# Second layer: 32 tokens gather the rows of their own experts, and work on gathered rows keeps its program order

## The chip, the cores and the metric

The kernel runs on one core of a Trainium2 chip as one launch. Its time is device microseconds (us); lower is better. Of the core's engines the text needs TensorE (PE in the profile, with its weight loads as PEld), VectorE (DVE), ScalarE (ACT), GpSimd (POOL, which issues the gathers) and SyncE (SP, a queue that issues loads). Sixteen DMA engines move data between HBM and the on-chip memory.

## What is computed

The model is two layers over 256 latent tokens (and, in the first layer, 256 context tokens). Each layer is a set of attention-like mixers and then an expert network, and it is the expert network that the change touches. Each token scores 8 x 2 x 128 keys, picks 128 of 16,384 experts (16 for each of 8 heads), and gets

```python
def peer_ffn(h, wq, sub_keys, u, v):
    ...
        fs, fpos = lax.top_k(cand_s, PEER_TOPK)
        eidx = jnp.take_along_axis(cand_i, fpos, axis=-1)
        gate = jax.nn.softmax(fs, axis=-1)
        act = jax.nn.gelu(jnp.einsum('td,thkd->thk', xb, u[eidx]).astype(F32), approximate=False)
        w = (gate * act).astype(xb.dtype)
        return jnp.einsum('thk,thkd->td', w, v[eidx])
```

Here `u` and `v` are tables of 16,384 rows of 1024 floats (64 MB each) for each layer. The first layer runs 512 tokens through this network, the second 256.

## The kernel before

There are two ways to do the expert network, and the kernel uses both.

**The dense way** computes every expert for every token and multiplies by a gate that is zero for the experts not chosen. The 16,384 experts are 128 blocks of 128. In the *u stage* (`u_blocks`, called in pairs by `u_pair`) each block of `u` is loaded (tile `raw`, 1 MB for two blocks, two buffers), split into a high part by a ScalarE copy and a low part by a VectorE subtraction (tiles `spl`, a ring of ten), and multiplied with the split activations `h2h`, `h2l`: eight chunks of the 1024 features, each as three fp32r products (`mm3`, lines 72 to 74), 24 products per block, into a PSUM tile `pu`. The moving operand has one column per token: `self.wd[l]` columns, 384 in the first layer and 256 in the second. A gelu goes to DRAM (`ad`), or for the first 40 blocks of the second layer stays in `kept`. In the *v stage* (`v_blocks`) the same is done with `v`: 128 blocks, again 24 products each of `wd[l]` columns, accumulated over all blocks in eight PSUM tiles `f0` to `f7`; the moving operand there is activation times gate (`va`, split into `wh` and `wl`).

The gate matrix is built while the u stage runs: `route` decodes which experts a token chose, and for groups of 8 tokens `gate_hot` builds one-hot tiles on VectorE (`bt`, `eq`, two `at`) and `gates` multiplies them on TensorE (tile `pg`, 16 fp16 products per group).

**The gathered way** (`tokens_apart`) takes only the 128 experts of each token. In the first layer, 128 tokens (one per partition) are set apart: for each of 128 slots a POOL indirect DMA gathers one row per partition (128 x 1024 floats, 512 KB), VectorE multiplies with the token's activation `ht` and sums (a *dot*, line 1384), and later another gather of `v` rows is scaled and added to `facc` (an *addition*, line 1391). In the u stage the gathered rows share the ring `spl`; in the v stage they have a ring `row` of four. The generator is advanced by `rows_to`: `PHASE1` steps are spread over the u stage, the rest over the first 58 pairs of the v stage. The second layer sets no tokens apart.

What sets the order: a scheduler places each engine's instructions by priority and by when it believes operands are ready. `pin` adds an edge that keeps an instruction behind everything written before it on its engine; it may still be placed later. Each engine then executes its list strictly in that order, so an instruction that waits holds up all behind it.

Of the kernel before, what the change touches and what calls it, by code (L numbers as in the profile page):

```python
# [18 lines left out]
L = 2  # L19
KD = 8  # L20
# [16 lines left out]
APART = 128  # L37
ROWS = 4
PHASE1 = 168
# [14 lines left out]
class Kernel:  # L54
# [39 lines left out]
    def build(self):  # L94
        tc, nc, A = self.tc, self.nc, self.A
        with ExitStack() as es:
# [25 lines left out]
            self.wd = [TA - APART, TC]  # L122
# [911 lines left out]
    def peer(self, l):  # L1034
# [5 lines left out]
        apart = (w - wd) // 128  # L1040
        with ExitStack() as es:
# [19 lines left out]
            with ExitStack() as e1:  # L1061
# [4 lines left out]
                with ExitStack() as e2:  # L1066
# [14 lines left out]
                    with self.order("DVE", "Activation"):  # L1081
                        self.pin(self.whigh(wr[0], ws[0], h0))
                        self.whigh(wr[0], ws[0], h1)
                        self.pin(self.wlow(wr[0], ws[0], h0))
                        scr = self.s.tile([128, 512], F32, name="s")
                        self.rs_diag(w, 1024, self.ms, scr)
                        self.wlow(wr[0], ws[0], h1)
                        self.norm2(aff, ts, hh, hl, self.rs_mm(w, scr, self.psum.tile([128, 512], F32, name="mm")), ht=ht)
# [10 lines left out]
                with ExitStack() as e2:  # L1099
# [12 lines left out]
                    if apart:  # L1112
                        for n, _ in enumerate(routes[0]):
                            if n % RN[l] == 0:
                                u_pair()
                        sp = self.tokens_apart(l, fin[0], ht)
                        next(sp)
                    first = apart
# [7 lines left out]
                    def u_next():  # L1126
                        u_pair()
                        rows_to(PHASE1 * (used[0] - u0) // (64 - u0))
                    for n, _ in enumerate(routes[first]):
                        if n % RN[l] == 0:  # L1130
                            u_next()
                    nd = nt - first
                    cost = [GW if t + 1 < nd else 1.0 for t in range(nd) for _ in range(16)]
                    left = 64 - used[0] - GL[l]
                    done = 0
                    sl = self.gate_slots(fin[first])
                    hot = self.gate_hot(sl, 0)
# [3 lines left out]
                    for x in range(16 * nd):  # L1141
                        t, g = divmod(x, 16)
                        while done < int(left * sum(cost[:x + 1]) / sum(cost) + 1e-6):
                            u_next()
                            done += 1
                        cur = hot
                        if t + 1 < nd:
                            next(routes[first + t + 1], None)
                            if g == 14:
                                for _ in routes[first + t + 1]:  # L1150
                                    pass
                                sl2 = self.gate_slots(fin[first + t + 1])
                            if g == 15:
                                sl = sl2
                        if x + 1 < 16 * nd:
                            hot = self.gate_hot(sl, (g + 1) % 16)
                        self.gates(l, t, g, cur)
# [4 lines left out]
                with ExitStack() as e2:  # L1162
# [16 lines left out]
                    for n, i in enumerate(self.v_order(l)):  # L1179
                        rows_to(PHASE1 + (256 - PHASE1) * n // 58 if n < 58 else 300)  # L1180
                        self.v_blocks(l, n, i, acc, ts, w - wd)
                        if extra:
                            self.ada_row(self.vp, *extra.pop(0))
# [3 lines left out]
    def norm2(self, aff, ts, hh, hl, rs, ks=range(KD), ht=None):  # L1187
# [12 lines left out]
        for k in ks:  # L1200
# [8 lines left out]
            if ht is not None:  # L1209
# [3 lines left out]
                nc.tensor.transpose(pt[:, c], t[:, 0:128], self.ident)  # L1213
                if k % 4 == 3:
                    nc.scalar.copy(ht[:, (k - 3) * 128:(k + 1) * 128], pt)
# [122 lines left out]
    def gates(self, l, t, g, hot):  # L1338
# [6 lines left out]
        for q in range(2):  # L1345
# [7 lines left out]
            if nf:  # L1353
                o = t * 128 + g * 8 + 4 * q
                f = self.kept[:, :, o:o + 4]
                nc.vector.scalar_tensor_tensor(f, pg[:, :nf], 1.0 / GSCALE, f, op0=ALU.mult, op1=ALU.mult)
        if g % 4 == 3:
            nc.scalar.dma_start(self.gd[l][4 * t + g // 4][:, nf:], self.gst)

    def tokens_apart(self, l, fin, ht):  # L1360
# [3 lines left out]
        ix = far.tile([128, 128], U32, name="ix")  # L1364
        fx = far.tile([128, 128], F32, name="fx")
        nc.vector.scalar_tensor_tensor(fx, fin[:, 0], 128.0, fin[:, 1], op0=ALU.mult, op1=ALU.add)
        nc.vector.tensor_copy(ix, fx)
        ga = far.tile([128, 128], F32, name="ga")
        nc.vector.tensor_copy(ga, fin[:, 2])
        dots = far.tile([128, 128], F32, name="dots")  # L1370
        wt = far.tile([128, 128], F32, name="wt")
        junk = self.junk = far.tile([128, 1024], F32, name="junk")
        self.facc = far.tile([128, 1024], F32, name="facc")
        tabs = [self.A[n].rearrange("a b d -> (a b) d") for n in (f"un{l}", f"vn{l}")]
# [5 lines left out]
        C = 16  # L1380

        def dot(s):
            r = gather(0, s)
            nc.vector.scalar_tensor_tensor(junk, r, 1.0, ht, op0=ALU.mult, op1=ALU.mult, accum_out=dots[:, s:s + 1])

        def add(s):
            r = gather(1, s)
            if s == 0:
                nc.vector.tensor_scalar(self.facc, r, wt[:, 0:1], None, op0=ALU.mult)
            else:  # L1390
                nc.vector.scalar_tensor_tensor(self.facc, r, wt[:, s:s + 1], self.facc, op0=ALU.mult, op1=ALU.add)
        yield
        for c in range(0, 128 + C, C):
            for s in range(c, c + C):
                if s < 128:
# [5 lines left out]
            if c < 128:  # L1401
# [48 lines left out]
    def v_blocks(self, l, n, i, acc, ts, off):  # L1450
# [41 lines left out]
        if off:  # L1492
# [6 lines left out]
        with self.order("PE", "DVE", "Activation"):  # L1499
# [3 lines left out]
            for d in range(KD):  # L1503
                mm(d, 1)
                if off:
                    nc.tensor.transpose(acc[d][:, 0:128], self.facc[:, d * 128:(d + 1) * 128], self.ident)
# [196 lines left out]
def layout(inp):  # L1703
# [46 lines left out]
    d["un0"], d["vn0"] = (f[x][0].reshape(128, 128, 1024) for x in ("peer_u", "peer_v"))  # L1750
# [19 lines left out]
```

## Time and profile before

| what | value |
|---|---|
| median of 3 runs | 2875.59 us (2870.84 to 2876.46) |
| profiled execution, device time | 2874.08 us |
| its span | 2872.0 us, 47065 instructions |
| TensorE busy | 2701.9 us (94%) |
| VectorE busy | 2178.1 us (76%) |
| ScalarE busy | 1265.1 us (44%) |
| GpSimd busy | 389.9 us (14%) |
| DMA | 662.88 MB, mean 231 GB/s |

The profiled execution is 1.5 us below the median of the runs. The span covers, in order: mixers of the first layer (to about 420 us), its expert network (to about 1765), mixers of the second layer (to about 2030), its expert network (to about 2865) and the output. A busy TensorE is not TensorE at its peak, since products overlap: the time that one product really costs is the distance between the starts of two that follow each other, called the pitch below.

### The profile page before, as it was taken

How to read it: one execution, taken by the hardware profiler on the slowest of the kernel's cores; microseconds unless marked ns; L12 is line 12 of the kernel's file. 1: busy time of each engine (PE TensorE's matmuls, PEld its weight loads, DVE VectorE, ACT ScalarE, POOL GpSimd, SP SyncE). 2: the span in 40 equal slices, each digit the busy share in tenths (PEclk: the TensorE clock that was granted, in tenths of full speed). 3: DMA queues.
4: the chain of work that ended last, by engine and by line, in shares of the span. 5: the costliest groups of instructions: out<-in, count | busy, mean ns of one | idle time of the engine just before them, and what ended most of it. 6: DMA issues, size and time to landing. Idle time of an engine off the chain costs nothing.

```text
span 2872.0 us, 47065 instructions
## 1 busy us (share of the span) xinstructions
PE 2701.9 (94%) x18199; PEld 2491.3 (87%) x18199; DVE 2178.1 (76%) x4703; ACT 1265.1 (44%) x2185; POOL 389.9 (14%) x354
## 2 busy tenths in 40 slices
PE   8989989999999987999999998988999999999998
PEld 5766758998888877999999997766999999999998
DVE  5665667689999976799999986655789767666665
ACT  5564644343344432343333334654545445444443
POOL 0010000004444343322222310000000000000000
PEclk9999899999999998999999999999999999999999
DMA  7111423237899999999999984211535766877774
GB/s 265 71 48 45 162 88 134 90 136 280 309 369 367 358 364 343 337 341 374 370 370 368 368 301 136 89 37 52 194 136 187 250 240 234 292 240 248 249 246 143
DMA packets 268752, 662.88 MB, mean 231 GB/s; under 512 B 16496, under 2 KB 146672, under 8 KB 258928
## 3 DMA queue, kind: packets, MB, share of 16 engines
q1 hardware_dynamic: 198688, 450.04, 45.0%
q0 software_dynamic: 36864, 134.23, 12.6%
q10 hardware_dynamic: 32976, 75.61, 6.9%
q8 instruction: 142, 2.33, 0.3%
q14 instruction: 82, 0.67, 0.1%
HBM read 585.37 MB, written 74.45 MB: 230 GB/s over the span
## 4 chain that ended last, share of the span: by engine, by line
PE 70%; DVE 16%; DMA 5%; issue 4%; ACT 3%; SPq 1%; POOL 0%; ACTq 0%; DVEq 0%; POOLq 0%
PE pu L72 8%; PE pu L74 8%; PE pu L73 8%; PE f L73 8%; PE f L74 8%; PE f L72 7%; PE fp L72 3%; PE fp L73 3%; PE fp L74 3%; PE pg L1349 2%; DVE junk L305 2%; DVE spl L1469 2%; PE mm L72 2%; PE mm L73 2%; PE mm L74 2%
## 5 line engine op out<-in xcount | busy, mean ns | idle before, releaser
L72 PE MATMUL pu<-h2h,spl 128*128 128x384 f32 (+1 forms) x2048 | 649.6, 317 | 39.4 <-ACT spl L1417 38.3
L73 PE MATMUL f<-wl,spl 128*128 128x384 f32 (+1 forms) x2048 | 635.3, 310 | 11.0 <-DVE wl L1476 11.0
L74 PE MATMUL pu<-h2h,spl 128*128 128x384 f32 (+1 forms) x2048 | 636.9, 313 | 8.2 <-DVE spl L1418 7.9
L73 PE MATMUL pu<-h2l,spl 128*128 128x384 f32 (+1 forms) x2048 | 639.4, 312 | 0.0
L74 PE MATMUL f<-wh,spl 128*128 128x384 f32 (+1 forms) x2048 | 629.2, 309 | 0.0
L72 PE MATMUL f<-wh,spl 128*128 128x384 f32 (+1 forms) x2048 | 511.7, 311 | 11.6 <-ACT wh L1475 8.4
L1468 ACT CAST spl<-raw 128x1024 fp32r<-128x1024 f32 x256 | 268.0, 1050 | 389.8 <-PE f L73 343.0
L72 PEld LDWEIGHTS pu<-h2h,spl 128*128 128x128 f32 x2048 | 393.0, 192 | 47.3 <-ACT spl L1417 44.0
L1469 DVE TENSOR_TENSOR spl<-raw,spl 128x1024 fp32r<-128x1024 f32 x256 | 312.6, 1225 | 158.8 <-ACT spl L1468 157.5
L1417 ACT CAST spl<-raw 128x1024 fp32r<-128x1024 f32 x256 | 266.6, 1049 | 343.1 <-PE pu L73 229.4
L73 PEld LDWEIGHTS f<-wl,spl 128*128 128x128 f32 x2048 | 389.7, 190 | 16.8 <-DVE wl L1476 16.1
L74 PEld LDWEIGHTS pu<-h2h,spl 128*128 128x128 f32 x2048 | 391.7, 191 | 12.7 <-DVE spl L1418 12.4
L1418 DVE TENSOR_TENSOR spl<-raw,spl 128x1024 fp32r<-128x1024 f32 x256 | 311.8, 1221 | 110.9 <-ACT spl L1417 108.8
L73 PEld LDWEIGHTS pu<-h2l,spl 128*128 128x128 f32 x2048 | 393.1, 192 | 0.3
L72 PEld LDWEIGHTS f<-wh,spl 128*128 128x128 f32 x2048 | 377.9, 190 | 16.1 <-ACT wh L1475 11.3
L74 PEld LDWEIGHTS f<-wh,spl 128*128 128x128 f32 x2048 | 389.2, 190 | 0.0
L418 DVE TENSOR_TENSOR spl<-raw,spl 128x512 fp32r<-128x512 f32 (+1 forms) x226 | 150.3, 704 | 72.7 <-ACT spl L414 62.5
L1435 ACT ACTIVATE act<-pu 128x384 f32<-128x384 f32 (+1 forms) x216 | 95.7, 443 | 218.7 <-PE pu L74 213.6
L1378 POOL DMA_INDIRECT spl<-in_un,ix x92 | 128.8, 1400 | 387.5 <-DVE fp L1246 244.0
L347 POOL TENSOR_TENSOR ms<-ms,mhalf 128x4 f32<-128x4 f32 (+1 forms) x5 | 4.8, 953 | 1264.1 <-DVE sq L345 833.9
L1475 ACT CAST wh<-va 128x384 fp32r<-128x384 f32 (+1 forms) x216 | 100.0, 467 | 168.5 <-PE f L74 79.5
L414 ACT CAST spl<-raw 128x512 fp32r<-128x512 f32 (+1 forms) x226 | 130.5, 629 | 76.8 <-PE fp L73 28.9
(305 smaller groups left out, 4547.6 us busy)
## 6 DMA issues: line engine op xcount, KB each, us to landing
raw<-in_ut SPq DMA_DIRECT2D x128, 1024.0 KB
raw<-in_v SPq DMA_DIRECT2D x128, 1024.0 KB
adaw<-in_wadat SPq DMA_DIRECT2D x56, 512.0 KB
ad<-act ACTq DMA_DIRECT2D x64, 384.0 KB
gd<-gstage ACTq DMA_DIRECT2D x12, 2048.0 KB
vg<-gd SPq DMA_DIRECT2D x32, 768.0 KB
va<-ad SPq DMA_DIRECT2D x64, 384.0 KB
raw<-in_win SPq DMA_DIRECT2D x22, 1024.0 KB
```

What stands on the lines that cost most here:

```text
L72: mm(ps, ah, bh, start=first, stop=False, **kw)
L73: mm(ps, ah, bl, start=False, stop=False, **kw)
L74: mm(ps, al, bh, start=False, stop=last, **kw)
L414: return self.nc.scalar.copy(p[0][o], w[:, o])
L418: return eng.tensor_tensor(p[1][o], w[:, o], p[0][o].bitcast(F32), op=ALU.subtract)
L1378: nc.gpsimd.indirect_dma_start(r, None, tabs[which], bass.IndirectOffsetOnAxis(ix[:, s:s + 1], 0))
L1417: self.pin(nc.scalar.copy(uh, self.u[:, n % 2]), n < 3)
L1418: self.pin(nc.vector.tensor_tensor(ul, self.u[:, n % 2], uh.bitcast(F32), op=ALU.subtract), n < 3)
L1435: nc.scalar.activation(a[:, b, :w], ps[:, :w], AF.Gelu)
L1468: nc.scalar.copy(vh, v[:, b])
L1469: nc.vector.tensor_tensor(vl, v[:, b], vh.bitcast(F32), op=ALU.subtract)
L1475: nc.scalar.copy(wh[:, :w], a[:, b, :w])
```

## The change

`APART` and `PHASE1` become a pair, one entry per layer. In the second layer the first 32 latent tokens are set apart. They fill the 128 partitions four times: partition 32q + t holds token t with slots 32q to 32q + 31, so there are 32 dots and 32 additions of 128 rows each (groups of 8 slots instead of 16). To get there, `ht` (32 rows) is copied three times by DMA, the routing result `fin` is rearranged into `own` by four DMAs, and the four partial sums are added at the end by a product with a 128 x 32 selection matrix `fsel`. All of these DMAs stand in SP's queue. The dense products of the second layer are then 224 columns wide, four groups of 8 tokens need no gate, and the activation and gate tiles in DRAM shrink likewise. In the first layer the last transposes of `facc` become products with the identity. In both layers each dot and each addition is pinned.

```diff
-APART = 128
+APART = (128, 32)
-PHASE1 = 168
+PHASE1 = (168, 26)
...
-            self.wd = [TA - APART, TC]
+            self.wd = [TA - APART[0], TC - APART[1]]
...
+                        for q in range(apart, 128, apart):
+                            nc.sync.dma_start(ht[q:q + apart], ht[0:apart])
...
-                nc.tensor.transpose(pt[:, c], t[:, 0:128], self.ident)
+                nc.tensor.transpose(pt[0:na, c], t[:, 0:na], self.ident)
...
+        if n < 128:
+            own = far.tile([128, 3, S], F32, name="own")
+            for q in range(128 // n):
+                nc.sync.dma_start(own[q * n:(q + 1) * n], fin[0:n, :, q * S:(q + 1) * S])
+            fin = own
+        self.fsel = self.ident
+        if n < 128:
+            self.fsel = far.tile([128, n], F32, name="fsel")
+            nc.vector.tensor_copy(self.fsel, self.ident[:, 0:n])
+            for q in range(n, 128, n):
+                nc.vector.tensor_add(self.fsel, self.fsel, self.ident[:, q:q + n])
...
-            nc.vector.scalar_tensor_tensor(junk, r, 1.0, ht, op0=ALU.mult, op1=ALU.mult, accum_out=dots[:, s:s + 1])
+            self.pin(nc.vector.scalar_tensor_tensor(junk, r, 1.0, ht, op0=ALU.mult, op1=ALU.mult, accum_out=dots[:, s:s + 1]))
...
-                nc.vector.scalar_tensor_tensor(self.facc, r, wt[:, s:s + 1], self.facc, op0=ALU.mult, op1=ALU.add)
+                self.pin(nc.vector.scalar_tensor_tensor(self.facc, r, wt[:, s:s + 1], self.facc, op0=ALU.mult, op1=ALU.add))
...
-                    nc.tensor.transpose(acc[d][:, 0:128], self.facc[:, d * 128:(d + 1) * 128], self.ident)
+                    nc.tensor.matmul(acc[d][:, 0:off], self.facc[:, d * 128:(d + 1) * 128], self.fsel, start=True, stop=True)
```

VectorE, v stage of the second layer, before (`spl` is the low part of a block, `wl` the low part of the weighted activations):

```order
L1469 TENSOR_TENSOR spl<-raw,spl 128x1024
L1476 TENSOR_TENSOR wl<-va,wh 128x256
L1474 TENSOR_TENSOR va<-va,vg 128x256 x2
L1469 TENSOR_TENSOR spl<-raw,spl 128x1024
L1476 TENSOR_TENSOR wl<-kept,wh 128x256
```

The same place in the changed kernel:

```order
L1399 SCALAR_TENSOR_TENSOR junk,dots<-row,ht 128x1024
L1484 TENSOR_TENSOR spl<-raw,spl 128x1024
L1491 TENSOR_TENSOR wl<-va,wh 128x224
L1484 TENSOR_TENSOR spl<-raw,spl 128x1024
L1491 TENSOR_TENSOR wl<-va,wh 128x224
L1489 TENSOR_TENSOR va<-va,vg 128x224 x2
L1484 TENSOR_TENSOR spl<-raw,spl 128x1024
L1491 TENSOR_TENSOR wl<-kept,wh 128x224
L1484 TENSOR_TENSOR spl<-raw,spl 128x1024
L1491 TENSOR_TENSOR wl<-kept,wh 128x224
L1406 SCALAR_TENSOR_TENSOR facc<-row,wt,facc 128x1024
```

Dots and additions now stand between the splits that feed TensorE; the first dot stands behind the split of block 55 of the u stage, the last addition behind that of block 126 of the v stage.

VectorE, v stage of the first layer, before (line 305 computes modulation rows of the next layer):

```order
L1474 TENSOR_TENSOR va<-va,vg 128x384 x2
L1469 TENSOR_TENSOR spl<-raw,spl 128x1024
L306 TENSOR_TENSOR mod_12303<-mod_12303,badat 128x2
L1384 SCALAR_TENSOR_TENSOR junk,dots<-row,ht 128x1024
L1476 TENSOR_TENSOR wl<-va,wh 128x384 x2
L305 SCALAR_TENSOR_TENSOR junk,mod_12303<-adaw,csb 128x1024
L1469 TENSOR_TENSOR spl<-raw,spl 128x1024
L305 SCALAR_TENSOR_TENSOR junk,mod_12303<-adaw,csb 128x1024
L1391 SCALAR_TENSOR_TENSOR facc<-row,wt,facc 128x1024
```

The same stage in the changed kernel:

```order
L1406 SCALAR_TENSOR_TENSOR facc<-row,wt,facc 128x1024
L1484 TENSOR_TENSOR spl<-raw,spl 128x1024
L305 SCALAR_TENSOR_TENSOR junk,mod_12303<-adaw,csb 128x1024
L1484 TENSOR_TENSOR spl<-raw,spl 128x1024
L1489 TENSOR_TENSOR va<-va,vg 128x384 x2
L305 SCALAR_TENSOR_TENSOR junk,mod_12303<-adaw,csb 128x1024
L1491 TENSOR_TENSOR wl<-va,wh 128x384 x2
L306 TENSOR_TENSOR mod_12303<-mod_12303,badat 128x2
L1399 SCALAR_TENSOR_TENSOR junk,dots<-row,ht 128x1024
L1406 SCALAR_TENSOR_TENSOR facc<-row,wt,facc 128x1024
```

The same instructions stand there in a more regular order; a dot moves by a few places, and the last addition goes from behind the split of block 116 to behind that of block 125.

SP, u stage of the second layer, in the changed kernel (`raw` are the loads of `u`):

```order
L1430 DMA raw_21530<-in_ut 128x2x1024
L1430 DMA raw_21594<-in_ut 128x2x1024
L1371 DMA own_21491<-fin0_19268 32x3x32 x4
L1430 DMA raw_21698<-in_ut 128x2x1024
L1430 DMA raw_21801<-in_ut 128x2x1024
```

The four rearranging DMAs wait for the routing result, and the loads of `u` stand behind them; before the change there were only loads of `u` there.

## Rows read from the trace of the kernel before

**Rows 1.** The page: busy engines, and the chain by engine.

```profile
PE 2701.9 (94%) x18199; PEld 2491.3 (87%) x18199; DVE 2178.1 (76%) x4703; ACT 1265.1 (44%) x2185; POOL 389.9 (14%) x354
...
PE 70%; DVE 16%; DMA 5%; issue 4%; ACT 3%; SPq 1%; POOL 0%; ACTq 0%; DVEq 0%; POOLq 0%
```

**Rows 2.** Second layer's stretches: length, busy PE, PEld, DVE, ACT, POOL, clock, DMA share, GB/s.

```profile
2120.00:2200.00 80.00, 80.00 (x667) 79.81 (x666) 73.44 (x278) 41.11 (x62) 0.00 (x0) 1.00 0.47 161
2360.00:2440.00 80.00, 80.00 (x754) 79.37 (x753) 60.00 (x91) 39.66 (x71) 0.00 (x0) 1.00 0.68 235
...
2640.00:2720.00 80.00, 80.00 (x669) 80.00 (x668) 49.97 (x75) 37.93 (x56) 0.00 (x0) 1.00 0.75 250
```

**Rows 3.** PE's largest wait in the second expert network: total, times, longest.

```profile
PE mm L356 <- DVE s L351: 3.9, 2, 2.1
```

**Rows 4.** PE in order of time: start, duration; second layer, first of 52 and last.

```profile
2599.77 0.28 PE L72 MATMUL f<-wh,spl 128*128 128x256 f32 x1
...
2605.89 0.28 PE L72 MATMUL f<-wh,spl 128*128 128x256 f32 x1
```

**Rows 5.** The same for the first layer, 384 columns, first of 15 and last.

```profile
553.30 0.34 PE L74 MATMUL pu<-h2h,spl 128*128 128x384 f32 x1
...
555.73 0.33 PE L73 MATMUL pu<-h2l,spl 128*128 128x384 f32 x1
```

**Rows 6.** PEld and PE in order of time: short moving operands.

```profile
14.24 0.52 PEld L285 LDWEIGHTS tp<-con,adarow 2*128 2x128 f32 x4 [0.44 <-issue]
...
551.78 1.50 PE L1236 MATMUL sk<-keys,s 128*128 128x128 f32 x12
...
2215.08 1.44 PE L1349 MATMUL pg<-at,bt 128*128 128x128 f16 x22
```

**Rows 7.** PE and PEld groups by line and form: busy, mean ns of one.

```profile
L72 PE MATMUL pu<-h2h,spl 128*128 128x256 f32 x1024 | 295.8, 289 | 0.0
...
L1236 PE MATMUL sk<-keys,s 128*128 128x128 f32 x192 | 25.9, 275 | 0.0
...
L1349 PEld LDWEIGHTS <-bt 128*128 128x128 f16 x1280 | 76.8, 99 | 24.2 <-issue 10.1 <-DVE at L1335 9.4 <-DVE bt L1332 0.6
...
L74 PEld LDWEIGHTS fp<-spl,s 128*128 128x128 f32 x128 | 24.6, 192 | 0.0
```

**Rows 8.** VectorE groups, second expert network: busy, mean ns of one.

```profile
L1335 DVE TENSOR_TENSOR at<-eq,parts 128x1024 f16<-128x1024 f16 x64 | 41.3, 685 | 0.0
L1476 DVE TENSOR_TENSOR wl<-va,wh 128x256 fp32r<-128x256 f32 x88 | 36.9, 419 | 3.6 <-ACT wh L1475 3.6
...
L1332 DVE TENSOR_TENSOR bt<-iob,slots 128x1024 f16<-128x1024 f16 x32 | 22.1, 692 | 40.5 <-PE pg L1349 40.5
...
L1356 DVE SCALAR_TENSOR_TENSOR kept<-pg,kept 128x160 f32<-128x160 f32 x64 | 18.5, 318 | 0.0
```

**Rows 9.** Gathered rows, first layer: ns min/median/max, first and last start.

```profile
L1384 DVE SCALAR_TENSOR_TENSOR junk<-row,ht x36: 1217/1222/1240, 1236.8 to 1622.2; 128x1024 f32<-128x1024 f32 x36
L1384 DVE DVE_READ_ACCUMULATOR junk<-row,ht x36: 81/86/104, 1238.0 to 1623.3; 128x1 f32 x36
...
L1391 DVE SCALAR_TENSOR_TENSOR facc<-row,wt,facc x52: 1279/1284/1298, 1219.6 to 1686.4; 128x1024 f32<-128x1024 f32 x52
```

**Rows 10.** The page's DMA queues: packets, MB, share; q0 carries the 256 gathers.

```profile
q0 software_dynamic: 36864, 134.23, 12.6%
```

**Rows 11.** The same as rows 2 in the first layer's u stage, v stage.

```profile
1000.00:1040.00 40.00, 36.41 (x268) 33.76 (x267) 38.94 (x53) 19.13 (x30) 15.05 (x11) 0.96 0.95 350
...
1480.00:1560.00 80.00, 76.42 (x432) 74.15 (x431) 79.14 (x128) 27.04 (x36) 19.52 (x15) 1.00 1.02 373
```

**Rows 12.** VectorE's largest wait for gathers, first layer's u stage.

```profile
DVE junk L1384 <- DMA spl<-in_un,ix: 9.0, 3, 4.4
```

## What the change will do: the prediction

> **What bounds the kernel now.** I read the page first. TensorE is busy for 94% of the span and carries 70% of the chain that ended last, VectorE 16% [rows 1]. A share over the whole span hides stages with different limits, so next I read the stretches of the stage that the change touches. In the u and v stages of the second layer TensorE is busy 80.00 us of every 80, at a granted clock of 1.00 (the 2.4 GHz level), VectorE 60.00 of 80 in the u stage and 49.97 of 80 in the v stage, and DMA at a share of 0.68 and 0.75 [rows 2]. Its largest wait in all of the second expert network is 3.9 us, in the norm at its end [rows 3]. So there TensorE alone sets the time: a microsecond that its list gets shorter is a microsecond of the span, as long as VectorE and DMA follow. The first layer is another matter: VectorE stands at 38.94 of 40 and 79.14 of 80 with DMA at 0.95 to 1.02, and TensorE is idle for 9% and 4.5% of those stretches [rows 11].
>
> **What a narrower product is worth.** The dense stages of the second layer are 2 x 128 blocks of 24 products, 6144 in all (1024 per line and stage, one of the six groups in [rows 7]). Their pitch at 256 columns is (2605.89 - 2599.77) / 51 = 0.120 us [rows 4]; at 384 columns it is (555.73 - 553.30) / 14 = 0.1736 us [rows 5]. The difference, 0.0536 us for 128 columns, is 0.42 ns per column, and what is left is a fixed 13 ns. If this line went on, 224 columns would cost 0.1066 us, and 6144 x 0.0134 = 82 us would be gone.
>
> But the line need not go on. Each product loads its own 128 x 128 weights, and where the moving operand is tiny the load itself can be seen: four loads for products of 2 columns take 0.52 us, which is (0.52 - 0.19) / 3 = 0.110 us from one to the next, and twelve f32 products of 128 columns stand (1.50 - 0.275) / 11 = 0.111 us apart [rows 6, 7]. fp16 loads are shorter, 99 ns against 192 ns for one [rows 7], and there the pitch goes down to 1.44 / 22 = 0.065 us or less [rows 6]. So a load of 4-byte weights appears to have a pitch of about 0.111 us of its own, which 256 columns hide and 224 don't. I take 0.111: it is the nearest row with the same kind of weights. The gain is then 6144 x 0.009 = **55 us**. Bounds: 0.1066 (82 us) if the load hides better than those rows show, and 0.120 (nothing) if the 13 ns come on top of the load too.
>
> The Trainium skill speaks for such a floor: "TensorE: Matmul & The Clock Gate", section "LDWEIGHTS (loading the stationary operand)", has the load take its columns over 1.2 GHz, whatever the number of rows, which for 128 columns is an estimate of 107 ns; by that alone the sum would have 80 us here instead of 55. The rows put the floor some 4 ns higher.
>
> **The rest of TensorE's list.** Four gate groups of 16 fp16 products go, 64 x 0.06 = 4 us. Eight transposes for `ht` come, and 16 products with `fsel` in the second layer, since an f32 product is two instructions, and 8 more in the first layer's end: 32 x 0.111 = 4 us, all of it on the path. These cancel.
>
> **VectorE.** Added are 32 dots of 1.222 + 0.086 us and 32 additions of 1.284 us [rows 9], 83 us. Removed are four gate groups, each 0.692 + 0.684 (the `eq`, the same shape) + 2 x 0.685 us, and 8 updates of `kept` at 0.318: 14 us. The 128 `wl` and 88 `va` operations of 0.419 us lose an eighth of their columns, at most 11 us [rows 8]. The net is some 60 us on an engine that waits for TensorE today. In the v stage its need per 80 us becomes 49.97 x 0.120 / 0.111 = 54, plus 38 of the 64 steps at 1.29 us over some 342 us, 11.5 per 80: 66 of 80. In the u stage the steps start behind block 55, so 26 of them fall into about 200 us, 13 per 80, and 60.00 x 1.08 + 13 - 5 gives 73 of 80 [rows 2]. That is 91%, under what the first layer runs at [rows 11]. The routing stretch, at 73.44 of 80 already, must run at 79 to keep up [rows 2]; I charge 2 us for it.
>
> **DMA.** 256 gathers took 134.23 MB and 12.6% of 2872 us [rows 10], so 64 take 33.6 MB and 90 us of all sixteen engines: 53 us in the v stage and 37 in the second half of the u stage. The shares become 0.75 x 1.08 + 53 / 342, less 0.03 for smaller activation tiles, = 0.94, and likewise 0.68 x 1.08 + 37 / 200 - 0.03 = 0.89. It fits, without much left.
>
> **Added waits.** The gathers wait for the routing result through `own`, four small DMAs in SP's queue with the `u` loads behind them; two `raw` buffers and five blocks of splits are TensorE's cover, over 10 us. A dot that waits for its row holds up the splits behind it; in the first layer, with DMA full, VectorE lost 9.0 us in three such waits over 92 dots [rows 12], and pinned dots stand no earlier than before. Nothing in the second layer prices these waits. Below, they cost nothing, since TensorE has the cover; above, what the first layer's v stage loses, 4.5% [rows 11], of some 500 us, 22 us. A gain is excluded, as TensorE has no idle time there to win back. I take 12 us with the 2 of routing in it, since the second layer has DMA at 0.9, not 1.0, and VectorE at 0.83 to 0.91, not 0.99.
>
> **First layer.** The pins move dots by a few places among the same instructions, in a stage where VectorE and DMA are full either way [rows 11]. I put it at 0, with 5 us to both sides, the size of the waits in [rows 12].
>
> **Sum.** -55 + 0 + 12 + 0 = -43 us. The profiled execution, 2874.1, becomes 2831; the median of the runs lies 1.5 us above it, so **2832 us**.
>
> **Rivals.**
> *Only columns count* (0.12): the pitch is 0.107 us, 80 us gone, stalls 14 as DMA is asked for more: 2874 - 66, with the 1.5, 2810. For it: 256 and 384 columns lie on a line. Against it: [rows 6].
> *The second layer becomes like the first* (0.13): dots and gathers hold up the splits, and TensorE idles by the 9% of the first layer's u stage [rows 11] over the 200 us with gathers and 4.5% over the v stage, 18 + 15 = 33 us, with the ring `spl` short by the rows it holds: 2853 to 2878. Against it: DMA has a tenth left.
> *The pitch stays at 0.120* (0.10): what paces the product is the load plus the 13 ns, and 256 columns already stand at that floor (0.107 + 0.013). Then narrowing gives nothing and only the 12 us of stalls remain: 2888 us, slower. It decides from a pitch of 0.118 on, where the gain no longer pays for the stalls. For it: nothing with 4-byte weights in [rows 4 to 6] but short ones is under 0.120; against it, those short ones, which have no 13 ns.
> *fp32r below 256 columns loses its rate* (0.04): no row shows a product of lines 72 to 74 with fewer columns than 256. If it ran at the pace of the f32 form, 2 x 0.111 us for 128 columns, that is 0.39 us for 224 and over 1600 us more. Nothing in the trace suggests it, and it stays out of the range.
> That the change doesn't do what it says can be left out: the changed order has the 128x224 forms and the dots.
>
> **How the numbers follow.** The forecast (0.61) spans 2815 to 2853, from a pitch of 0.109 with few stalls to 0.112 with 25 us of them. What a measurement can tell from no change is about 0.2%, 6 us. Faster by more: the forecast 0.61, only columns 0.12, two thirds of the second rival 0.08, together 0.81. Slower by more: 0.10 x 0.7 + 0.04 = 0.11. Within: 0.08. The range goes from 2808, under the case of columns alone, to 2882, which takes in the second rival and the better part of the third; about 0.06 is left below and 0.11 above.
>
> **What would show it.** In the profile after, the start-to-start distance of the products in the second layer's v stage should be 0.111 us; 0.107 or 0.120 decides for a rival. TensorE should stay above 97% busy there, with its waits naming the splits (`spl`), `wl` or `wh` where it does not. VectorE should be near 66 of 80 in the v stage and 73 in the u stage, DMA near 0.9; waits of VectorE for gathers should be a few us. The first layer should end within 5 us of where it did. The prediction is wrong if the pitch is not 0.109 to 0.113, or if TensorE idles more than 25 us in the second layer.

## The result: 2844 us, 0.990 of before

The changed kernel takes 2844.06 us in the median of 4 runs (2842.68 to 2853.02). The ratio to before, 2876.03 us in the same comparison, is 0.9897 with a 95% interval of 0.9872 to 0.9922: 30 us faster. The profiled execution took 2844.33 us with a span of 2842.6. Single executions of one and the same kernel scatter by some 10 us, so below a ratio is taken for the time, and the profile for where it lies.

First the page: busy engines, and the two largest DMA queues (packets, MB, share of sixteen engines; q0 carries the gathers). They answer to [rows 1, 10].

```profile
PE 2661.0 (94%) x18167; PEld 2447.5 (86%) x18167; DVE 2230.5 (78%) x4786; ACT 1256.0 (44%) x2183; POOL 481.9 (17%) x418
...
q1 hardware_dynamic: 196464, 447.60, 44.9%
q0 software_dynamic: 46080, 167.79, 16.0%
```

The gathers moved 33.6 MB more than before, as worked out. Next, two products of the second layer's v stage in order of time (start, duration), 17 pitches apart with no gap between; they answer to [rows 4].

```profile
2649.80 0.28 PE L73 MATMUL f<-wl,spl 128*128 128x224 f32 x1
...
2651.70 0.27 PE L72 MATMUL f<-wh,spl 128*128 128x224 f32 x1
```

1.90 / 17 = 0.112 us: the floor that the prediction put at 0.111. Then the stretches, with the columns of [rows 2]: two of the u stage, three of the v stage.

```profile
2120.00:2200.00 80.00, 78.05 (x697) 77.68 (x696) 77.49 (x270) 44.70 (x67) 2.49 (x1) 1.00 0.55 184
2360.00:2440.00 80.00, 77.04 (x760) 76.45 (x759) 68.50 (x101) 41.46 (x74) 11.81 (x7) 1.00 0.83 290
...
2480.00:2560.00 80.00, 76.84 (x676) 75.68 (x675) 60.10 (x90) 38.42 (x57) 11.40 (x9) 1.00 0.88 308
2560.00:2640.00 80.00, 75.93 (x664) 74.53 (x663) 56.72 (x86) 35.89 (x57) 11.58 (x9) 1.00 0.86 296
2640.00:2720.00 80.00, 79.80 (x713) 79.53 (x713) 63.07 (x97) 38.86 (x60) 9.10 (x10) 1.00 0.95 322
```

TensorE no longer stands at 80.00. Its count of products says more than its busy time, as busy products overlap: the kernel without gathered work, below, makes 719 in such a stretch of the v stage, so 676 and 664 mean 4.8 and 6.1 us lost, where the busy time shows 3.2 and 4.1. Last, the waits in the v stage: the engine and line, what it waited for, the total, how often, the longest.

```profile
PE f L73 <- DVE wl L1491: 5.8, 9, 1.6
...
ACT spl L1483 <- DMA raw<-in_v: 124.4, 49, 4.9
...
DVE va L1489 <- DMA va<-ad: 33.5, 19, 3.6
```

Before the change, ScalarE's waits in the v stage (2500 to 2820) were these:

```profile
ACT spl L1468 <- PE f L73: 157.7, 105, 1.5
ACT spl L1468 <- DMA raw<-in_v: 8.4, 4, 2.7
```

TensorE itself shows few waits, but the split on ScalarE, which used to wait for TensorE, now waits 49 times for the load of its block. So the place to look is the loads.

The length of a stage, here and in the table further on, is the distance between the first and the last product of line 73 in it, as in these rows of the changed kernel (count, duration in ns, first and last start): first layer's v stage, second layer's u stage and v stage.

```profile
L73 PE MATMUL f<-wl,spl x1024: 331/334/446, 1204.0 to 1757.7; 128*128 128x384 f32 x171
...
L73 PE MATMUL pu<-h2l,spl x1024: 269/274/352, 2040.8 to 2462.9; 128*128 128x224 f32 x171
...
L73 PE MATMUL f<-wl,spl x1024: 268/275/420, 2465.6 to 2829.0; 128*128 128x224 f32 x171
```

Against before, the first layer's v stage is 11.0 us shorter, the second layer's u stage 19.0 and its v stage 6.2; the way from the first layer to the second, the step from u to v stage and the end grew by 2.2, 2.3 and 1.3 us. The v stage, from which the prediction had 3072 x 0.009 = 28 us, gave 6, and the first layer, from which it had nothing, gave 11.

### The profile page after: what moved, and what is told of

It reads as the page before. It is cut to its first block, busy times and chain, and to the rows that moved or that the text cites. A ratio compares the mean times of both kernels' runs of the same rounds, so it can differ in the third digit from the quotient of the medians.

```text
span 2842.6 us, 47140 instructions
## 1 busy us (share of the span) xinstructions
PE 2661.0 (94%) x18167; PEld 2447.5 (86%) x18167; DVE 2230.5 (78%) x4786; ACT 1256.0 (44%) x2183; POOL 481.9 (17%) x418
## 5 line engine op out<-in xcount | busy, mean ns | idle before, releaser
L72 PE MATMUL pu<-h2h,spl 128*128 128x384 f32 (+1 forms) x2048 | 638.5, 312 | 48.9 <-ACT spl L1432 35.1
L73 PE MATMUL f<-wl,spl 128*128 128x384 f32 (+1 forms) x2048 | 623.4, 307 | 12.2 <-DVE wl L1491 11.8
L74 PE MATMUL pu<-h2h,spl 128*128 128x384 f32 (+1 forms) x2048 | 628.2, 308 | 5.5 <-DVE spl L1433 5.3
L73 PE MATMUL pu<-h2l,spl 128*128 128x384 f32 (+1 forms) x2048 | 630.6, 308 | 0.0
L74 PE MATMUL f<-wh,spl 128*128 128x384 f32 (+1 forms) x2048 | 607.8, 305 | 0.4 <-DVE spl L1484 0.3
L72 PE MATMUL f<-wh,spl 128*128 128x384 f32 (+1 forms) x2048 | 506.1, 307 | 12.4 <-ACT spl L1483 5.1
L1393 POOL DMA_INDIRECT spl<-in_un,ix x109 | 144.1, 1322 | 732.9 <-DVE fp L1248 243.2
L1393 POOL DMA_INDIRECT row<-in_vn,ix x75 | 113.1, 1507 | 366.4 <-DVE facc L1406 323.4
```

The source lines that it names most:

```text
L72: mm(ps, ah, bh, start=first, stop=False, **kw)
L73: mm(ps, ah, bl, start=False, stop=False, **kw)
L74: mm(ps, al, bh, start=False, stop=last, **kw)
L1393: nc.gpsimd.indirect_dma_start(r, None, tabs[which], bass.IndirectOffsetOnAxis(ix[:, s:s + 1], 0))
```

## Experiments

Three questions: is the floor really 0.112 us, what eats the v stage's gain (VectorE's added work, or the transfers), and what do the pins do? All stage lengths in one table (us), each from the one profiled execution of its kernel:

| kernel | ratio to before | first layer v | second layer u | second layer v |
|---|---|---|---|---|
| before | 1 | 564.7 | 441.1 | 369.6 |
| changed | 0.9897 | 553.7 | 422.1 | 363.4 |
| changed, again | 0.9906 | 553.7 | 422.9 | 362.6 |
| pins alone | 0.9938 | 552.9 | 441.1 | 369.6 |
| change without pins | 1.0007 | 565.4 | 427.0 | 374.9 |
| pins in first layer only | 0.9964 | 554.0 | 425.2 | 376.1 |
| 224 columns, no gathered work | 0.9797 | 553.7 | 414.7 | 345.5 |
| dots and additions, no gathers | 0.9792 | 553.6 | 414.5 | 345.6 |
| 192 columns, no gathered work | 0.9779 | 553.6 | 411.6 | 346.6 |
| gathers, thin dots | 0.9902 | 553.6 | 431.0 | 359.0 |
| gathers of 64 columns | 0.9858 | 554.1 | 423.7 | 350.4 |
| all gathers in the v stage | 0.9916 | 553.7 | 416.5 | 383.5 |
| 16 tokens | 0.9869 | 553.7 | 432.0 | 355.1 |
| 16 tokens, gathers in the v stage | 0.9875 | 554.0 | 416.6 | 366.6 |

### The changed kernel again, beside the others

> The changed kernel once more, as the mark for the others. Expected 2844 us, within 2840 to 2853; second layer's products 0.112 us apart, its v stage some 364 us long.

Measured: 2844.35 us (2837.36 to 2852.63), ratio 0.9906 (0.9890 to 0.9923). It is the yardstick for the runs below.

### Pins alone, on the kernel before

```diff
-            nc.vector.scalar_tensor_tensor(junk, r, 1.0, ht, ..., accum_out=dots[:, s:s + 1])
+            self.pin(nc.vector.scalar_tensor_tensor(junk, r, 1.0, ht, ..., accum_out=dots[:, s:s + 1]))
```

and the same for the two forms of the addition.

> The kernel before with the pins on dots and additions and nothing else. If the pins are what shortened the first layer's v stage from 565 to 554 us, this run has that stage at 554 +- 3 us and 2866 us in all (2862 to 2870). Rival: the 11 us came from something else in the first layer or from one execution; then 2876 +- 3 us and a stage of 565.

Measured: 2854.36 us, 0.9938 (0.9926 to 0.9951): 18 us, and less than the 2862 to 2870 us that were expected, while the stage came to 552.9 as expected: the profile shows 11.8 us there (the profiled execution was 9 us above the median, so the rest isn't placed). The prediction had put the pins at 0, with 5 us to both sides. Where it comes from is looked for in the stretches of that stage, columns as above; first the kernel before, 1560 to 1640 and 1680 to 1720:

```profile
1560.00:1640.00 80.00, 75.99 (x432) 74.30 (x431) 76.70 (x124) 26.50 (x37) 25.02 (x16) 1.00 1.01 359
...
1680.00:1720.00 40.00, 38.13 (x218) 37.81 (x219) 30.52 (x48) 13.98 (x20) 0.00 (x0) 1.00 0.81 255
```

and the changed kernel, which has the same order there as pins alone:

```profile
1480.00:1560.00 80.00, 79.12 (x452) 77.72 (x451) 79.19 (x128) 27.80 (x38) 24.70 (x14) 1.00 1.03 375
1560.00:1640.00 80.00, 80.00 (x457) 78.42 (x455) 79.49 (x127) 28.60 (x39) 27.20 (x16) 1.00 1.03 377
...
1680.00:1720.00 40.00, 39.11 (x224) 38.43 (x223) 37.40 (x53) 13.52 (x19) 7.32 (x5) 1.00 0.92 320
...
L1406 DVE SCALAR_TENSOR_TENSOR facc<-row,wt,facc x52: 1271/1278/1285, 1246.3 to 1712.0; 128x1024 f32<-128x1024 f32 x52
```

The last row has the additions, with first and last start, and answers to [rows 9]. Before, the gathers were over by 1680 (GpSimd 0.00), and VectorE and DMA had slack behind that. With pins the additions start until 1712.0 instead of 1686.4, and 457 products fit where 432 did. The queue of VectorE was full in the middle of the stage and not at its end; the pins use the end. That is not all of it: from 1480 to 1560 VectorE is as busy before [rows 11] as with pins, 79.14 and 79.19 us in 128 instructions, and yet TensorE makes 452 products in place of 432. How much is due to the later end and how much to the more regular order, these runs do not tell apart.

### The change without pins

```diff
-            self.pin(nc.vector.scalar_tensor_tensor(junk, r, 1.0, ht, ..., accum_out=dots[:, s:s + 1]))
+            nc.vector.scalar_tensor_tensor(junk, r, 1.0, ht, ..., accum_out=dots[:, s:s + 1])
```

and so for the additions.

> The changed kernel without the pins. If they gave 8 to 11 us in the first layer and nothing in the second: 2853 us (2850 to 2857), first v stage 565 us. Rival, that they don't matter: 2844 us. Second rival, that in the second layer they hold back splits and cost there: under 2844 us.

Measured: 2874.91 us, 1.0007 (0.9997 to 1.0017). That is above all three expectations (2853, 2844, under 2844): without pins the tokens apart give nothing at all. The first layer's v stage came to 565.4 as expected, so what was not foreseen lies in the second layer. The second layer's v stage takes 374.9 us, more than the 369.6 at 256 columns. Its stretches:

```profile
2480.00:2560.00 80.00, 67.70 (x549) 66.42 (x550) 67.63 (x101) 30.47 (x48) 32.25 (x23) 0.94 1.04 380
2560.00:2640.00 80.00, 71.75 (x596) 70.15 (x595) 62.01 (x89) 35.15 (x53) 15.10 (x12) 0.96 0.87 308
2640.00:2720.00 80.00, 80.00 (x719) 80.00 (x718) 53.37 (x84) 40.23 (x62) 0.00 (x0) 1.00 0.79 262
```

The scheduler pulled the dots and additions forward: 23 gathers in the first 80 us against 9 with pins, DMA at 1.04, TensorE down to 549 products, and nothing left to gather from 2640 on, when 719 products pass. The same 64 gathers, bunched, cost all that the narrower products give.

A part of this is TensorE's clock. The granted clock is 0.94 and 0.96 in these two stretches, where the changed kernel has 1.00. After TensorE had waited 3.6 us up to 2482.7, it fell to 0.50 (the 1.2 GHz level); here beside a stretch of the same length at the 2.4 GHz level:

```profile
2484.00:2489.00 5.00, 5.00 (x24) 5.00 (x25) 3.11 (x4) 0.00 (x0) 0.00 (x0) 0.50 1.09 359
2640.00:2645.00 5.00, 5.00 (x48) 5.00 (x47) 4.37 (x8) 3.18 (x6) 0.00 (x0) 1.00 0.83 270
```

At the lower level half as many products are made. As an estimate, the two mean clocks mean (0.06 + 0.04) x 80 / 0.5 = 16 us at the lower level and some 8 us lost, of the 29.3 that the v stage lost against the kernel without gathers below.

### Pins in the first layer only

```diff
-            self.pin(nc.vector.scalar_tensor_tensor(junk, r, 1.0, ht, ..., accum_out=dots[:, s:s + 1]))
+            self.pin(nc.vector.scalar_tensor_tensor(junk, r, 1.0, ht, ..., accum_out=dots[:, s:s + 1]), l == 0)
```

> The changed kernel with the dots and additions pinned in the first layer alone. Theory A, the pins are worth some 12 us in the first layer and some 18 us in the second, so the first v stage stays at 554 us, the second v stage goes to 375 us as without any pins, 0.996 to 0.997 of before, 2861 us. Theory B, nearly all of the 30 us come from the first layer: 0.991, 2845 us.

Measured: 2861.86 us, 0.9964 (0.9952 to 0.9976), as theory A had it: (1.0007 - 0.9964) x 2872 = 12 us of the pins come from the first layer and (0.9964 - 0.9906) x 2872 = 17 us from the second, each uncertain by some 5 us by the intervals.

### 224 columns, no gathered work

The 32 tokens still have no dense work, and in the second layer all gathers, dots and additions are left out. The lines stand in `tokens_apart`, ahead of its steps.

```diff
+        if l == 1:
+            nc.vector.memset(self.facc, 0.0)
+            return
```

> The changed kernel without the gathers, dots and additions of the second layer; the 32 tokens' expert part is left out. What is left of the change is the narrower product. If the 31 us that TensorE lost against its new pitch come from the gathered work (by DMA or by VectorE): 2815 us (2810 to 2820), v stage 345 us, products 0.112 us apart. Rival: the narrower products themselves stall, since loads and splits must keep a faster pace; then 2835 to 2844 us.

Measured: 2814.92 us, 0.9797 (0.9784 to 0.9809). Against pins alone, the second layer's stages lose 26.4 and 24.1 us, together 50.5, and the pitch accounts for some 6144 x 0.008 = 49 of it.

### Dots and additions without gathers

In the second layer the gathers are left out; the dots and additions all run, on the tile `ht` in place of a row. The lines stand in `gather`.

```diff
+            if l == 1:
+                return ht
```

> The changed kernel, but in the second layer each dot and addition reads the resident tile ht in place of a gathered row: 64 gathers, 33.6 MB and the places that rows take in the ring are gone, VectorE's work and its order stay, and the 32 tokens' result is left wrong. The gathered work costs 28 us (2844 against 2815 us with none of it). If DMA and late rows are the cause: 2818 us (2813 to 2824), v stage 348 us. If VectorE's 83 us are: 2840 us (2834 to 2846), v stage 360 us.

Measured: 2809.95 us, 0.9792 (0.9775 to 0.9808), the same as without any gathered work, and less than either expectation had (2813 to 2824, 2834 to 2846). VectorE's order did not quite stay: the scheduler, with no rows to wait for, put the first dot at 2186.8 and the last addition at 2752.5, against 2204.1 and 2789.2 in the changed kernel. A stretch of its v stage, and ScalarE's waits in the v stage and, last, in the u stage from 2200 on:

```profile
2560.00:2640.00 80.00, 80.00 (x719) 80.00 (x718) 61.87 (x96) 39.68 (x60) 0.00 (x0) 1.00 0.78 258
```

```profile
ACT spl L1485 <- PE f L73: 134.9, 103, 1.4
ACT spl L1485 <- DMA raw<-in_v: 16.0, 8, 3.3
...
ACT spl L1434 <- DMA raw<-in_ut: 11.3, 6, 2.6
```

TensorE makes its 719 products, and ScalarE waits for TensorE, as it should where TensorE is the bound. VectorE has its dots and additions (61.87 of 80) and costs nothing. The whole price of the tokens apart is in the gathers, with the ring places and the waits that come with them: (0.9906 - 0.9792) x 2872 = 33 us between this kernel and the changed one, uncertain by some 7 us.

### Gathers kept, dots and additions on 64 of 1024 columns

The rows are fetched whole, but in the second layer dots and additions work on 64 columns; the rest is left out.

```diff
+        W = 64 if l else 1024
...
-            self.pin(nc.vector.scalar_tensor_tensor(junk, r, 1.0, ht, ...))
+            self.pin(nc.vector.scalar_tensor_tensor(junk[:, :W], r[:, :W], 1.0, ht[:, :W], ...))
```

> The changed kernel with all gathers of the second layer, but dots and additions there read only 64 of the 1024 columns, so that VectorE loses most of its 83 us; the 32 tokens' result is left wrong. If DMA is the cause: 2840 us (2835 to 2846). If VectorE is: 2818 us (2813 to 2824). Both near 2830 would mean that each takes a share.

Measured: 2843.04 us, 0.9902 (0.9885 to 0.9918), the same as the changed kernel. Taking VectorE's work away and leaving the gathers gives nothing; taking the gathers away and leaving the work gives everything. Within this total the u stage is 8 to 9 us longer and the v stage 4 shorter. The scheduler orders VectorE's instructions anew in this kernel, so its stages are not those of the changed kernel with thinner dots. And the granted clock is 0.98 in each of the three stretches of the u stage from 2200 to 2440, here the middle one, where the changed kernel has 1.00 in all three:

```profile
2280.00:2360.00 80.00, 76.83 (x729) 76.30 (x728) 54.21 (x87) 36.52 (x65) 7.85 (x7) 0.98 0.84 288
```

By the same estimate that is some 5 us of the u stage; the rest, and the 4 us, stay open.

### 192 columns, no gathered work

```diff
-APART = (128, 32)
+APART = (128, 64)
```

on top of the run with 224 columns and no gathered work; 64 tokens have neither dense nor gathered work.

> As narrow_only (no gathered work in the second layer), but with 64 tokens left out, so that the products are 192 columns wide. If the load of the weights sets a floor of 0.112 us: products still 0.112 us apart and 2811 us (2805 to 2815), the 4 us less for four more gate groups. If columns set the pitch after all: 0.093 us apart and some 115 us less, 2700 us.

Measured: 2807.69 us, 0.9779 (0.9763 to 0.9795). In order of time, again 17 pitches:

```profile
2649.83 0.28 PE L74 MATMUL f<-wh,spl 128*128 128x192 f32 x1
...
2651.74 0.27 PE L73 MATMUL f<-wl,spl 128*128 128x192 f32 x1
```

1.91 / 17 = 0.112 us, the same as at 224 columns. So at 224 columns the pitch has reached a floor, and fewer columns are worth nothing. That the load of the weights makes this floor is concluded from the short products with 4-byte weights, which stand as far apart [rows 6]; no run changes the load alone.

### Gathers of 64 columns

Each gather of the second layer fetches 256 bytes per partition instead of 4 KB, out of the table cut into pieces of 64 columns. Number of gathers, ring places and waits stay; dots and additions work on 64 columns, as in the run with thin dots, which is therefore the nearest comparison.

```diff
-            nc.gpsimd.indirect_dma_start(r, None, tabs[which], bass.IndirectOffsetOnAxis(ix[:, s:s + 1], 0))
+            few = self.A[("un1", "vn1")[which]].rearrange("a b (c e) -> (a b c) e", e=64)
+            nc.gpsimd.indirect_dma_start(r[:, :64], None, few, bass.IndirectOffsetOnAxis(ix[:, s:s + 1], 0))
```

> The changed kernel, but each gather of the second layer fetches only 64 of the 1024 columns of a row into its tile (dots and additions work on these 64 columns; the rest of the gathered product is left out). The number of gathers, their tiles in the rings and their waits stay. Theory A, the bytes of the gathers are what delays the loads of blocks: a sixteenth of the bytes, the second layer's u stage comes near 416 us and its v stage near 347 us as without gathers, 0.980 of before, 2814 us. Theory B, the number of descriptors, the places in the rings or the waits: u stage 423 or more, v stage 358 or more, 0.990, 2842 us.

Measured: 2830.1 us, 0.9858 (0.9839 to 0.9877), 13 us less than with thin dots and whole rows. In the v stage it is the bytes: 350.4 us against 359.0 with thin dots and 345.6 without gathers, and ScalarE's waits turn back to TensorE:

```profile
ACT spl L1490 <- PE f L73: 114.1, 90, 1.4
ACT spl L1490 <- DMA raw<-in_v: 34.5, 18, 3.7
```

VectorE's wait for the activations `va`, 33.5 us in the changed kernel, is 11.9 us here and 11.8 without gathers, so it is not only the blocks of `v` that the bytes delay.

In the u stage most of the price is still there with a sixteenth of the bytes: 423.7 us, 9 more than without gathers. The changed kernel has 422.1, but the run with thin dots 431.0, so these runs do not settle whether the bytes have a share there too. The waits are those of the changed kernel; first GpSimd, ScalarE and VectorE of the changed kernel, then GpSimd and ScalarE of this one, from 2200 to 2465:

```profile
POOL spl L1393 <- PE pu L74: 173.2, 20, 12.9
...
ACT spl L1432 <- DMA raw<-in_ut: 67.2, 31, 6.0
...
DVE junk L1399 <- DMA spl<-in_un,ix: 13.4, 5, 4.1
...
DVE facc L1406 <- DMA spl<-in_vn,ix: 5.4, 3, 2.4
```

```profile
POOL spl L1395 <- PE pu L74: 188.9, 21, 16.9
ACT spl L1439 <- DMA raw<-in_ut: 73.7, 28, 7.5
```

The gathered rows share the ring `spl` with the splits there. GpSimd waits for a place until TensorE has used up a split. The likely reading is that the splits behind are late by that, and so are the loads into the two `raw` buffers that the splits free, so that the wait for `raw` is here an effect of the ring: it is 73.7 us with small gathers, 67.2 with whole rows and 11.3 without gathers. Whether it is the place itself or the dot waiting for its row ahead of the splits, these runs do not tell apart; no run gives the rows a ring of their own in the u stage.

### All gathers in the v stage

```diff
-PHASE1 = (168, 26)
+PHASE1 = (168, 0)
```

> The changed kernel with all 64 gathers of the second layer in its v stage and none in its u stage. Theory A, a gather costs the same stall wherever it stands (18 us for 38 in the v stage, 0.47 us each): u stage 415 us, v stage 376 us, 0.992 of before, 2848 us. Theory B, stalls grow steeply as the DMA engines fill up (a share of 0.77 plus 90 us in 360, 1.02): v stage 390 us or more, 0.996 or more, 2860 us. Theory C, in the u stage it is the ring places taken from the splits that cost, and a ring of their own in the v stage hides the gathers: u stage 415, v stage 366, 0.988, 2838 us.

Measured: 2850.95 us, 0.9916 (0.9897 to 0.9934). The u stage comes back to 416.5 us, so its loss belongs to the gathers in it; the v stage goes to 383.5, between theories A and B. There 64 gathers cost 383.5 - 345.6 = 38 us, 0.59 each, against 0.47 each for the 38 of the changed kernel (the profiled execution was the longest of this kernel, 2858.3, so that is rather too much). A part of the difference is the clock again: granted 0.97, 0.96 and 0.98 in the three stretches from 2480 to 2720, 1.00 in the changed kernel. By the estimate used above that is some 7 us, and without them 31 / 64 = 0.48 each, which is theory A's price. A ring of their own does not hide them (theory C fell). In total nothing is won: the ratio is that of the changed kernel within the intervals.

### 16 tokens

If columns are free below the floor, 16 tokens should buy nearly the same pitch with half the bytes. For want of room `FOLD` goes from 20 to 18.

```diff
-FOLD, QS, VA = (0, 20), (10, 6), (2, 3)
+FOLD, QS, VA = (0, 18), (10, 6), (2, 3)
...
-APART = (128, 32)
+APART = (128, 16)
...
-PHASE1 = (168, 26)
+PHASE1 = (168, 13)
```

> The changed kernel with 16 tokens set apart in place of 32: 240 columns, whose price by columns (0.113 us) is just above the floor of the weight load, and half the gathers, dots and additions. (The ring of gates in DRAM keeps groups of 32 tokens, and 36 blocks in place of 40 stay in kept, for lack of room.) If gathered work costs in proportion: 8 us lost on the pitch, 14 won: 2838 us (2832 to 2844). If its price is mostly that of starting at all: 2850 us.

Measured: 2834.38 us (2833.2 to 2846.7), 0.9869 (0.9852 to 0.9885), by the ratios 10 us faster than the changed kernel (0.9906) and 1.3% faster than before. The pitch at 240 columns, over 16 products in order of time, and a stretch of the v stage:

```profile
2649.75 0.27 PE L73 MATMUL f<-wl,spl 128*128 128x240 f32 x1
...
2651.55 0.28 PE L74 MATMUL f<-wh,spl 128*128 128x240 f32 x1
...
2640.00:2720.00 80.00, 80.00 (x713) 80.00 (x712) 58.65 (x107) 39.51 (x60) 6.11 (x5) 1.00 0.87 299
```

is 1.80 / 16 = 0.1125 us, and with TensorE busy throughout, 713 products stand where 224 columns had 719. So 240 columns lie just above the floor: 0.0009 us per product, some 6 us over the 6144. The profiled execution was the slowest, 2846.7, so its 432.0 us for the u stage are likely more than the other executions had.

### 16 tokens, all gathers in the v stage

The run above with `PHASE1 = (168, 0)`.

> 16 tokens apart as in the run with 16 tokens, but with all 32 of its gathers in the second layer's v stage and none in its u stage. If gathers cost the u stage ring places and the v stage bytes, the u stage comes down from 432 to some 416 us, and the v stage with 32 gathers at 0.5 to 0.6 us each goes to 362 to 365 us: 0.9835 of before, 2825 us, faster than with 16 tokens and gathers in both stages (0.9869). If it is the number of gathers alone, wherever they stand, nothing changes: 0.987, 2835 us.

Measured: 2837.15 us, 0.9875 (0.9859 to 0.9892): a miss. The u stage came to 416.6 us as expected, but 32 gathers made the v stage 366.6 us, not 362 to 365, and the total is that of the run above within its interval. Where gathers stand matters little. Against the kernel without gathers these two kernels lose (0.9875 - 0.9792) x 2872 = 24 us and 22 us, where the changed kernel loses 33. Not all of it is gathers: some 6 us are the wider product. The expectation counted from the 345.6 us of 224 columns; 345.6 x 719 / 713 = 348.5 us is the base at 240, and with it the measured 366.6 is 0.57 us for each gather, within its 0.5 to 0.6. Some 3 to 5 us more are the clock by the estimate used above (granted 0.98 in two stretches of the u stage in the run above, in three of the v stage in this one). That leaves 13 us for half the gathers, near half of the 28 to 33 for all.

## Why the prediction held, and where its steps failed

The forecast was 2832 us, the measurement 2844, within the range and on the side that was forecast. But of the four terms of its sum two were off, with opposite signs, so that the number came out so near is in part luck: 16 us or more too few for the stalls against 12 us that the pins gave in the first layer and that were put at 0. Without those 12 us it would have been some 2856, above the forecast's own 2815 to 2853, if within the whole range. And without pins in either layer nothing would have been gained (1.0007).

**The pitch: right.** 0.112 against 0.111 us, with the floor of short 4-byte loads [rows 6] as the reason, and the 192-column run shows that it is a floor. Some -49 instead of -55 us. The rivals "only columns count" (0.107) and "the pitch stays" (0.120) both fell. The Trainium skill's page "TensorE: Matmul & The Clock Gate", section "LDWEIGHTS (loading the stationary operand)", has a load take its columns over 1.2 GHz, for 128 columns an estimate of 107 ns; the traces put the pitch some 5 ns higher.

**Gates, transposes, `fsel`: not contradicted.** The way into the second layer grew by 2.2 us, of 4 worked out for all added products. The end grew by 1.3 us, but the kernel without gathers has the same products with `fsel` and its end did not grow, so that is not their price. The gates' gain can't be told apart within the u stage.

**The stalls: mis-sized.** 12 us were taken, with 22 as the upper bound. The profile of the changed kernel has 7.6 us in the u stage, 17.8 in the v stage and 2.4 more between them over the kernel without gathers, 28 us, and by the ratios it is 33 (in the profiles the first layer's u stage, with the same instructions, differs by another 4 to 7 us between these two kernels, and by 3.5 us between two executions of the changed kernel; I can't explain it). The step that failed is the bound: "above, what the first layer's v stage loses, 4.5%", and the choice below it because DMA would stand at 0.9 and not 1.0. DMA came out about as worked out, 0.83 to 0.95, and VectorE a little below, 68.50 of 80 in the u stage (73 forecast) and 63.07 in the v stage (66). It is the reading of the shares that was wrong: a mean share under 1 was taken for room. In the v stage the bytes of the gathers delay the loads of blocks and activations, and with two `raw` buffers such a delay reaches ScalarE's split, then TensorE. The cover of "over 10 us" was counted for a queue that is ahead, but ScalarE had long stopped being ahead: it waited 49 times for its block. And in the u stage the gathered rows take places in the very ring that was counted as cover, which is the likely reason there, not a shown one. What TensorE's clock costs after a wait was not in the sum at all; in the changed kernel that is little: of the stretches of these two stages only the one from 2440 to 2480 has a granted clock below 1.00 (0.96).

**The rival "becomes like the first"** had the size of the stalls right (33 us), though it gave 18 to the u stage and 15 to the v stage, where the profile has 8 and 18. Of its cause the gathers held and the dots did not: VectorE's work without gathers proved free.

**The first layer: wrong.** The pins were put at 0 because the stage is full either way [rows 11]. It is full in the middle and not at its end; pins keep the scheduler from doing the additions early and make the order more regular, and 12 us came out. In the second layer they are worth 17 more, which the prediction counted nowhere: the profile without pins has 12.5 + 29.3 + 3.9 = 46 us of stalls in the second layer, counted in the same way, and no gain is left. Some 8 us of these are the clock, by the estimate above.

**By the named checks:** pitch within 0.109 to 0.113, yes. TensorE over 97% busy in the v stage: 96, 95 and 99.8% in the stretches shown, and by its products 94, 92 and 99%; no. First layer within 5 us: no, 10 us earlier. Waits of VectorE for gathers a few us: 13.4 us for dots and 5.4 for additions in the u stage, none in the v stage. The idle time of TensorE in the second layer, named with 25 us as a sign of being wrong, is 788.20 - 765.88 = 22 us from the first product of line 73 in the u stage to the last in the v stage:

```profile
2040.80:2829.00 788.20, 765.88 (x6945) 758.99 (x6944) 616.62 (x1224) 382.54 (x625) 82.20 (x64) 1.00 0.77 268
```

So the sign did not appear. Busy time hides a part, since overlapping products count as busy: measured against the kernel without gathers, the stages and the step between them lost 28 us.

## What to carry to other kernels

Before narrowing an operand, look for the floor of the weight load in short products of the same type: once it is reached, further columns gain nothing, so take the smallest step that comes near it. Price an added transfer by whose load it delays and how many buffers stand between, not by whether the mean DMA share stays under 1, and do not let it share the ring that you count as cover. A step that holds work in program order is not free of consequence even where an engine looks full: compare the stage's middle with its end, and price the order by a run of its own. Where an engine's stalls grow, read the granted clock beside them, since a stall here cost more than its own length when the clock fell after it.

## What the runs showed of the hardware beyond expectation

Products with 4-byte weights of 128 x 128 have a pitch of 0.112 us at 224 and at 192 columns; 256 columns stand at 0.120 [rows 4]. After a wait of 3.6 us in the kernel without pins the granted clock fell from 1.00 to 0.50, and TensorE made 24 products in 5 us instead of 48. The mean DMA share is a poor measure of what just-in-time loads suffer: at 0.86 to 0.88 with gathers among the 1 MB loads TensorE made 664 to 676 products of 719 in 80 us, at 0.95 in the next stretch 713, and at 0.78 without gathers all 719. Of arbitration the Trainium skill's page "DMA: Bandwidth & Descriptors", section "Queues, rings and completion order", says that each engine goes round the queues that have work, a packet at a time; that fits a gather delaying a load issued before it, but no row here shows the order of packets.
